# The reciprocal of attention's row sums by way of DRAM, and the first norm's squares summed on VectorE

## The chip, the cores and the metric

The kernel runs on one NeuronCore of a Trainium2 chip. The metric is the device time of one execution in microseconds (us). A NeuronCore has a matrix engine (TensorE, PE in the rows; its weight loads are listed as PEld), VectorE (DVE), ScalarE (ACT), GpSimd (POOL) and SyncE (SP), which here only issues DMAs. Each engine works through its own instructions in order and waits on semaphores for the others.

## The reference

Two layers of a transformer-like trunk over 512 latent and 256 context tokens of width 1024. What matters here:

- Each layer begins with an RMS norm over the 1024 channels, x / sqrt(mean(x^2) + eps), scaled and shifted per channel by values that a matrix product makes from a conditioning vector (the modulation).
- One projection feeds three mixers: a gated delta rule in chunks (GDN), grouped-query attention with 8 heads of 64 channels and 2 key heads, and a short convolution. Their outputs are joined and projected back.
- Attention is softmax(q k^T / 8) v: the exponentials of a row are divided by their sum.
- Then comes a second norm with a SwiGLU network (layer 0) or experts (layer 1).

## The kernel before, in words

Activations lie with channels on partitions and tokens along the free dimension. Most products are made of three matmuls over a high and a low part of each operand (`parts`, `split`: L207 on ACT, L208 on DVE). A framework writes the order of each engine's instructions when the kernel is built: it walks them by priority, which is the order of the program, with its own estimates of durations, and places an instruction when its inputs and its buffer are free by these. On the chip that order is fixed. A load that is placed on SP ahead of another one is issued ahead of it, and one that waits (for a buffer, or for data) holds everything behind it on SP.

**First stage** (`start`, L444 to L492). SP loads modulation weights (groups 2 and 3), the eight tiles of x (128 channels by 768 tokens each), more modulation weights (groups 0 and 1) and the first projection weights. `stats` (L325) sums the squares of a segment of tokens over channels: even tiles are squared on ACT (L339), odd ones on DVE (L337), each square is summed over its 128 partitions by a matmul with ones into four strips of PSUM (L341), the strips are copied (L344), transposed and added up (L347). `rsq` (L234) makes the reciprocal root in 12 small DVE instructions (L239 to L246), and a diagonal matrix times ones (L352, L357) spreads the result over all partitions. `start` runs this for the 512 latent tokens (L479), scales the first 256 of them (`scaled`, L362 on DVE), runs it for the 256 context tokens (L481), and then for each half of the channels makes the modulation (`mod`: L265 on PE) and shifts (`shifted`: L367 on ACT, L368 on DVE). The rest of the tokens follows, and then the first projection (L221 to L223 on PE).

The kernel has a second way to norm, used further on: `square` (L370) squares on ACT and adds on GpSimd into an accumulator (k = 0 and, with two accumulators, k = 7 are written directly), and `rms` (L380) sums the accumulator with one-column matmuls (L387) into PSUM, from which `rsq` reads.

**Attention** (`Mix.attention`, L1496) runs as a generator beside GDN: both are woven together so that attention's work fills PE. The unit is two heads of one pair of query tiles (2 x 128 queries): 12 units in layer 0, 8 in layer 1. `scores` (L1560) makes for each of the two heads and two tiles the scores S (L1572, L1573), the row minimum of the negated scores on DVE (L1574) and the exponentials with their sums on ACT (L1575); the sums lie in `st[:, 1]`, one number per query on its partition, four columns for two heads and two tiles. One unit later `turn` transposes the exponentials (L231, copies L1531), and `values` multiplies with v (L1546); the result has the channels of two heads on the partitions and the queries along the free dimension. So 1 / sum, which is made per query on partitions, is needed along the free dimension, on all 64 partitions of its head. Before, this went over PE: DVE takes the reciprocal (L1535), GpSimd spreads it on four diagonals (L1536), PE multiplies ones with them (L1549) into the second half of the same PSUM bank, ACT copies this to `a_rs` (L1552), and DVE multiplies (L1553, into `a_y`). After that product the bank is free for the next transposes (there are two banks "t").

What else goes through the queues in these stages: in layer 0 six groups of modulation (4 to 9) are made between the units, each with four loads of 512 KB on SP (L196) through three buffers and with L265 on PE. In layer 1 SP has no loads in the attention stage until the output weights. GpSimd issues the loads of q, k, v and of GDN's right sides (L1878).

Of the kernel before, what the change touches and what calls it, by code (L numbers as in the profile page):

```python
# [8 lines left out]
F32 = mybir.dt.float32  # L9
F32R = mybir.dt.float32r  # L10
I32 = mybir.dt.int32
AF = mybir.ActivationFunctionType
# [5 lines left out]
SEGS = ((0, 512), (512, 256))  # L18
# [118 lines left out]
class K:  # L137
# [75 lines left out]
    def mm3(self, out, wh, wl, xh, xl, start, stop):  # L213
        mm = self.nc.tensor.matmul
        mm(out, wh, xh, start=start, stop=False)  # L215
        mm(out, wh, xl, start=False, stop=False)  # L216
        mm(out, wl, xh, start=False, stop=stop)  # L217

    def mm3x(self, out, xh, xl, wh, wl, start, stop):
        mm = self.nc.tensor.matmul  # L220
        mm(out, xh, wh, start=start, stop=False)  # L221
        mm(out, xl, wh, start=False, stop=False)  # L222
        mm(out, xh, wl, start=False, stop=stop)  # L223
# [143 lines left out]
        self.nc.scalar.activation(a, t, AF.Identity, bias=sh)  # L367
        self.nc.vector.scalar_tensor_tensor(b, t, sh, a.bitcast(F32), op0=OP.add, op1=OP.subtract)  # L368

    def square(self, pool, acc, xs, k):  # L370

        nc = self.nc
        if k == 0 or k == 7 and len(acc) > 1:
            nc.scalar.activation(acc[k // 7], xs, AF.Square)
            return
        sq = pool.tile([128, 512], F32, name="sq")[:, :xs.shape[-1]]
        nc.scalar.activation(sq, xs, AF.Square)
        nc.gpsimd.tensor_add(acc[0], acc[0], sq)

    def rms(self, pool, acc, n, b, dg=None):  # L380

# [50 lines left out]
def pools(k, l):  # L432

    def opener(side):
        return lambda es, n, bufs=1: es.enter_context(k.tc.tile_pool(name=n, bufs=bufs, side=side, reuse_waits="tile"))
    r = [opener("left"), opener("right")]
    return r if l == 0 else r[::-1]


def htiles(pool):  # L440
    return [[pool.tile([128, T], F32R, name=f"h{x}{i}") for i in range(8)] for x in "hl"]


def start(k):  # L444
    nc = k.nc
    pa, pb = pools(k, 0)
    eh = ExitStack()
    hh, hl = htiles(pa(eh, "hp"))
    with ExitStack() as es:
        np_ = pb(es, "np", 2)  # L450
        k.weights(es, 0, pb, 12)
        k.banks(es, pn=4, ps=2, pt=2)
        k.mod_begin(0, "pt")
        for g in (2, 3):
            k.mod(0, g, "ps", "pt")
        gain = k.gains(0, 0)
        x = []
        for i in range(8):
            t = np_.tile([128, T], F32, name=f"x{i}", bufs=1)
            nc.sync.dma_start(t, k.xsrc[0][:, i])  # L460
            x.append(t)
        sh = [np_.tile([128, 2, 4], F32, name=f"sh{g}", bufs=1) for g in range(2)]
        rs = {}

        def scaled(s, c, n):
            o = SEGS[s][0]
            for i in range(8):
                k.scaled(x[i][:, o + c:o + c + n], x, s, o + c, n, gain, rs[s][:, c:c + n], i)

        def shifted(s, c, n, ks=range(8)):  # L470
            o = SEGS[s][0] + c
            for i in ks:
                k.shifted(x[i][:, o:o + n], hh, hl, s, o, n, sh[i // 4], -4 * (i // 4), i)

        def mod(g):
            k.mod(0, g, "ps", "pt")
            nc.vector.tensor_copy(sh[g], k.modc[0][:, :, 4 * g:4 * g + 4])

        rs[0], = k.stats(np_, x, SEGS[:1])  # L479
        scaled(0, 0, 256)  # L480
        rs[1], = k.stats(np_, x, SEGS[1:])  # L481
        for g in range(2):
            mod(g)
            shifted(0, 0, 256, range(4 * g, 4 * g + 4))
        ep = ExitStack()
        k.weights(ep, 5, pa, 2)
        w0 = group_weights(k, 0, 1)
        scaled(0, 256, 256)
        shifted(0, 256, 256)
        scaled(1, 0, CTX)  # L490
        shifted(1, 0, CTX)
    return hh, hl, eh, ep, w0  # L492
# [47 lines left out]
def group_weights(k, l, i):  # L540
    n = 2 * WGN[i]
    return [k.weight(k.A[f"wg{i}"][l, q].rearrange("p k n -> p (k n)"), n) for q in range(4)]
# [794 lines left out]
class Mix:  # L1337
# [158 lines left out]
    def attention(self, sp, cat, groups):  # L1496

        k, nc = self.k, self.k.nc
        w, late, n = self.w, None, 0
        for g in range(2):  # L1500
            kh, v = self.first if g == 0 else self.keys(g)
            for h in (4 * g, 4 * g + 2):
                q = self.queries(h) if h else self.q0
                yb = sp.tile([128, w], F32, name="a_y", bufs=1)
                for pair in range(2 if self.last else 3):
                    kts = list(range(NT)) if pair < 2 else [4, 5]
                    st = sp.tile([128, 3, 4], F32, name="a_st", bufs=3)
                    P, pt = [], []
                    for i in range(2):
                        P.append(self.scores(sp, q[i], kh, pair, kts, st, 2 * i))  # L1510
                        if late:
                            self.turn(sp, i, *late)
                        if late and i:
                            self.values(sp, cat, *late)
                        yield
                        n += 1
                        if groups and n % 3 == 0:
                            k.mod(0, groups.pop(0), "t", "t")
                    late = h, pair, kts, P, v, yb, st, pt
        for i in range(2):  # L1520
            self.turn(sp, i, *late)
        self.values(sp, cat, *late)

    def turn(self, sp, j, h, pair, kts, P, v, yb, st, pt):

        k, nc = self.k, self.k.nc
        pt.append(sp.tile([128, NT, 256], F32, name="a_pt"))
        for a in range(0, len(kts), 2):
            tp = k.transposes([P[j][i][:, b * 128:b * 128 + 128] for b in (a, a + 1) for i in range(2)], b="t")
            tp = tp.rearrange("p (t q) -> p t q", t=2)  # L1530
            (nc.vector.tensor_copy if DVE_COPY[self.l] and a == 2 else nc.scalar.copy)(pt[j][:, kts[a]:kts[a] + 2], tp)  # L1531
        if j:

            dg = sp.tile([128, 4, 128], F32, name="a_dg", bufs=1)
            nc.vector.reciprocal(st[:, 2], st[:, 1])  # L1535
            nc.gpsimd.tensor_mul(dg, k.C("ident").unsqueeze(1).to_broadcast([128, 4, 128]),  # L1536
                                 st[:, 2].unsqueeze(2).to_broadcast([128, 4, 128]))
            pt.append(dg)

    def values(self, sp, cat, h, pair, kts, P, v, yb, st, pt):  # L1540

        k, nc, w = self.k, self.k.nc, self.w
        op = k.psum("t")
        for a, t in enumerate(kts):
            for j in range(2):
                nc.tensor.matmul(op[64 * j:64 * j + 64, :256], v[:, t], pt[j][:, t], start=a == 0, stop=a == len(kts) - 1,  # L1546
                                 tile_position=(0, 64 * j))
        for j in range(2):
            nc.tensor.matmul(op[64 * j:64 * j + 64, 256:], k.C("ones")[:, :64],  # L1549
                             pt[2][:, 2 * j:2 * j + 2].rearrange("p i q -> p (i q)"), start=True, stop=True, tile_position=(0, 64 * j))  # L1550
        rs = sp.tile([128, 256], F32, name="a_rs", bufs=1)
        nc.scalar.activation(rs, op[:, 256:], AF.Copy)  # L1552
        nc.vector.tensor_mul(yb[:, pair * 256:pair * 256 + 256], op[:, :256], rs)  # L1553
        if pair == (1 if self.last else 2):
            if 2 + h // 2 in cat:
                k.parts(yb[:, :w], *cat[2 + h // 2])
            else:
                nc.gpsimd.dma_start(self.cat[2 + h // 2, :, :w], yb[:, :w])
# [21 lines left out]
class Gdn:  # L1580
# [64 lines left out]
    def norm(self):  # L1645

        k, nc, ss = self.k, self.k.nc, self.ss
        k.rsq(self.p0, ss, [128, 2, NT, 4], 1.0, EPS, ss, "g")
        nc.vector.tensor_scalar(ss[:, 1], ss[:, 1], 0.125, None, op0=OP.mult)
        for w in range(2):  # L1650
            tok = self.tk[w]
            nc.vector.tensor_mul(tok, tok, ss[:, w].unsqueeze(3).to_broadcast([128, NT, 4, 64]))
            nc.gpsimd.dma_start(self.tok[1 - w], tok)
# [326 lines left out]
```

## Time and profile before

| | us |
|---|---|
| runs, median of 3 | 2132.27 (2132.15, 2132.27, 2135.34) |
| profiled execution | 2134.24 |
| its span in the profile | 2132.5 |
| PE busy | 2011.8 (94%) |
| DVE busy | 1398.4 (66%) |
| ACT busy | 996.0 (47%) |
| POOL busy | 229.5 (11%) |

How to read the rows further down. A row of the timeline gives start and length in us from the span's start, the engine, the line, the operation, what it writes and reads, how many instructions were merged, and in brackets how long the engine had been idle and what ended that. A row of a table of stretches gives the stretch, its length, then the busy time (and the number of instructions) of PE, PEld, DVE, ACT and POOL, the granted clock of PE as a share of 2.4 GHz, the busy share of the DMA engines and GB/s. A row of waits gives who waited for whom, us in total, times, and the longest. A row of one line gives the count, the shortest, median and longest ns, and the first and last start. A row of groups gives count, busy us, mean ns, and the idle time before. SPq is SP's queue. A matmul in full precision is shown as two instructions.

### The profile page before, as it was taken

Reading aid. Unit: us, or ns where it says so; the run is one execution under the profiler, and the core shown is the slowest. Engines: PE = TensorE matmul, PEld = TensorE weight load, DVE = VectorE, ACT = ScalarE, POOL = GpSimd, SP = SyncE. Lnnn points to the kernel's source line nnn. Section 1 sums busy time; section 2 is a strip of 40 time slices with the busy share of each in tenths; the row PEclk is TensorE's granted clock in tenths of the full one; section 3 lists DMA queues with packets and bytes.
Section 4 is the critical chain, followed back from the end, with each engine's and each line's share of the span. In section 5 each row is a group of like instructions: output and inputs, shape, how many; then the busy total and the mean of one; then the engine's idle time right before and its main releaser. Section 6 shows DMA issues by size and latency. Waiting matters only on the chain. (4 is left out here: it accounts for less than half of the span.)

```text
span 2132.5 us, 33501 instructions
## 1 busy us (share of the span) xinstructions
PE 2011.8 (94%) x12422; PEld 1647.2 (77%) x12422; DVE 1398.4 (66%) x2501; ACT 996.0 (47%) x1748; POOL 229.5 (11%) x276
## 2 busy tenths in 40 slices
PE   6999899989999999999989998999789999999996
PEld 2998766768788888888879886778567777777774
DVE  3858855765896734242367598677576788666777
ACT  3665375543322222222246556654365576645555
POOL 0000222214000000000040004210110000000011
PEclk9999999999999999999999999999899999999998
DMA  6342543152564715131233333034597799667674
GB/s 260 93 134 70 166 163 115 33 172 93 197 207 129 246 42 206 33 102 50 69 123 108 102 102 117 22 117 146 168 327 255 257 353 332 214 222 240 241 277 157
DMA packets 123489, 344.56 MB, mean 162 GB/s; under 512 B 13280, under 2 KB 36816, under 8 KB 123312
## 3 DMA queue, kind: packets, MB, share of 16 engines
q1 hardware_dynamic: 81216, 273.85, 38.3%
q0 software_dynamic: 14608, 47.87, 6.7%
q10 hardware_dynamic: 27488, 20.52, 3.1%
q8 instruction: 106, 1.74, 0.3%
q14 instruction: 71, 0.58, 0.1%
HBM read 306.00 MB, written 36.19 MB: 160 GB/s over the span
## 5 line engine op out<-in xcount | busy, mean ns | idle before, releaser
L207 ACT ACTIVATE hi<-raw 128x1024 fp32r<-128x1024 f32 (+3 forms) x444 | 426.2, 987 | 302.2 <-PE ps L216 230.7
L208 DVE TENSOR_TENSOR lo<-raw,hi 128x1024 fp32r<-128x1024 f32 (+2 forms) x432 | 482.7, 1138 | 85.5 <-ACT hi L207 69.5
L215 PE MATMUL ps<-hh,hi 128*128 128x512 f32 (+1 forms) x1040 | 355.8, 342 | 0.8 <-ACT hi L207 0.8
L217 PE MATMUL ps<-hh,lo 128*128 128x512 f32 (+1 forms) x1040 | 353.9, 340 | 1.7 <-DVE lo L208 1.7
L216 PE MATMUL ps<-hl,hi 128*128 128x512 f32 (+1 forms) x1040 | 354.6, 341 | 0.0
L215 PEld LDWEIGHTS ps<-hh,hi 128*128 128x128 f32 x1040 | 198.2, 191 | 26.7 <-ACT hi L207 3.4
L217 PEld LDWEIGHTS ps<-hh,lo 128*128 128x128 f32 x1040 | 198.1, 190 | 24.2 <-DVE lo L208 2.5
L216 PEld LDWEIGHTS ps<-hl,hi 128*128 128x128 f32 x1040 | 198.3, 191 | 21.2
L223 PE MATMUL ps<-lo,xh 128*128 128x512 f32 (+1 forms) x384 | 150.6, 393 | 10.7 <-DVE lo L208 5.1
L221 PE MATMUL ps<-hi,xh 128*128 128x512 f32 (+1 forms) x384 | 145.9, 380 | 2.0 <-ACT hi L207 1.9
L222 PE MATMUL ps<-hi,xl 128*128 128x512 f32 (+1 forms) x384 | 144.7, 377 | 0.0
L1332 DVE TENSOR_TENSOR sg<-sg,ps 128x512 f32<-128x512 f32 (+1 forms) x44 | 24.4, 554 | 150.7 <-PE ps L217 150.7
L217 PE MATMUL ps<-gh,lo 128*128 128x256 f32 (+1 forms) x352 | 119.2, 338 | 2.8 <-DVE lo L208 2.8
L216 PE MATMUL ps<-gl,hi 128*128 128x256 f32 (+1 forms) x352 | 120.2, 342 | 0.0
L215 PE MATMUL ps<-gh,hi 128*128 128x256 f32 (+1 forms) x352 | 119.2, 339 | 0.0
L223 PEld LDWEIGHTS ps<-lo,xh 128*128 128x128 f32 x384 | 72.4, 189 | 38.7 <-DVE lo L208 16.5
L296 DVE SCALAR_TENSOR_TENSOR macc<-mraw,sT,macc 128x512 f32<-128x512 f32 x126 | 89.4, 749 | 13.7 <-DMA mraw<-wmod 12.8
L221 PE MATMUL ps<-hi,hh 128*128 128x400 f32 (+2 forms) x272 | 91.7, 338 | 1.3 <-ACT hi L207 1.1
L223 PE MATMUL ps<-lo,hh 128*128 128x400 f32 (+2 forms) x272 | 89.3, 330 | 0.6 <-DVE lo L208 0.6
L222 PE MATMUL ps<-hi,hl 128*128 128x400 f32 (+2 forms) x272 | 88.4, 326 | 0.0
L1574 DVE TENSOR_REDUCE a_st<-S 128x1 f32<-128x768 f32 (+1 forms) x80 | 66.2, 844 | 31.2 <-PE S L1573 30.8
L1575 ACT ACTIVATE a_p<-S,a_st 128x768 f32<-128x768 f32 (+1 forms) x80 | 65.1, 816 | 43.3 <-DVE a_st L1574 38.9
(594 smaller groups left out, 4140.4 us busy)
## 6 DMA issues: line engine op xcount, KB each, us to landing
raw<-wmg SPq DMA_DIRECT2D x176, 512.0 KB
raw<-wmd SPq DMA_DIRECT2D x80, 512.0 KB
raw<-wmod SPq DMA_DIRECT2D x48, 512.0 KB
mraw<-wmod SPq DMA_DIRECT2D x48, 512.0 KB
raw<-wgu SPq DMA_DIRECT2D x44, 512.0 KB
raw<-wout SPq DMA_DIRECT2D x32, 512.0 KB
raw<-wt SPq DMA_DIRECT2D x24, 512.0 KB
raw<-wd SPq DMA_DIRECT2D x32, 256.0 KB
```

The source lines that it names most:

```text
L207: self.nc.scalar.activation(hi, src, AF.Copy)
L208: (eng or self.nc.vector).tensor_sub(lo, src, hi.bitcast(F32))
L215: mm(out, wh, xh, start=start, stop=False)
L216: mm(out, wh, xl, start=False, stop=False)
L217: mm(out, wl, xh, start=False, stop=stop)
L221: mm(out, xh, wh, start=start, stop=False)
L222: mm(out, xl, wh, start=False, stop=False)
L223: mm(out, xh, wl, start=False, stop=stop)
L296: nc.vector.scalar_tensor_tensor(a, w, c, a, op0=OP.mult, op1=OP.add)
L1332: nc.vector.tensor_mul(s, s, pu)
L1574: nc.vector.tensor_reduce(st[:, 0, c + i:c + i + 1], s[:, :n], axis=AX.X, op=OP.min)
L1575: nc.scalar.activation(P[:, :n], s[:, :n], AF.Exp, bias=st[:, 0, c + i:c + i + 1], scale=-1.0, accum_out=st[:, 1, c + i:c + i + 1])
```

## The change

In attention the reciprocals of a unit are taken as soon as its scores are done, written to a row in DRAM (two heads of 256 queries) and read back twice, each head's row to the 64 partitions of that head. All three DMAs are issued by SP. The diagonal, its matmuls and the copy fall away. In `start` the latent and the context norm are made by `square` and `rms`, with the additions on VectorE in place of GpSimd, and the context's norm stands behind the first shifts.

```diff
-    def square(self, pool, acc, xs, k):
+    def square(self, pool, acc, xs, k, eng=None):
...
-        nc.gpsimd.tensor_add(acc[0], acc[0], sq)
+        (eng or nc.gpsimd).tensor_add(acc[0], acc[0], sq)
...
-        rs[0], = k.stats(np_, x, SEGS[:1])
+        def norm(s):
+            o, n = SEGS[s]
+            acc = [np_.tile([128, 512], F32, name=f"nac{i}")[:, :n] for i in range(2)]
+            for i in range(8):
+                k.square(np_, acc, x[i][:, o:o + n], i, nc.vector)
+            rs[s] = k.rms(np_, acc, n, "pn")
+
+        norm(0)
         scaled(0, 0, 256)
-        rs[1], = k.stats(np_, x, SEGS[1:])
         for g in range(2):
             mod(g)
             shifted(0, 0, 256, range(4 * g, 4 * g + 4))
+        norm(1)
...
-                    late = h, pair, kts, P, v, yb, st, pt
+                    late = h, pair, kts, P, v, yb, self.sums(sp, st, h, pair), pt
...
+    def sums(self, sp, st, h, pair):
+
+        k, nc = self.k, self.k.nc
+        nc.vector.reciprocal(st[:, 2], st[:, 1])
+        row = k.dram.tile([2, 256], F32, name=f"rs{self.l}_{h}_{pair}")
+        nc.sync.dma_start(row.rearrange("j (i p) -> p (j i)", p=128), st[:, 2])
+        rs = sp.tile([128, 256], F32, name="a_rs", bufs=3)
+        for j in range(2):
+            nc.sync.dma_start(rs[64 * j:64 * j + 64], row[j].partition_broadcast(64))
+        return rs
+
-    def turn(self, sp, j, h, pair, kts, P, v, yb, st, pt):
+    def turn(self, sp, j, h, pair, kts, P, v, yb, rs, pt):
...
-        if j:
-
-            dg = sp.tile([128, 4, 128], F32, name="a_dg", bufs=1)
-            nc.vector.reciprocal(st[:, 2], st[:, 1])
-            nc.gpsimd.tensor_mul(dg, k.C("ident").unsqueeze(1).to_broadcast([128, 4, 128]),
-                                 st[:, 2].unsqueeze(2).to_broadcast([128, 4, 128]))
-            pt.append(dg)
-
-    def values(self, sp, cat, h, pair, kts, P, v, yb, st, pt):
+
+    def values(self, sp, cat, h, pair, kts, P, v, yb, rs, pt):
...
-        for j in range(2):
-            nc.tensor.matmul(op[64 * j:64 * j + 64, 256:], k.C("ones")[:, :64],
-                             pt[2][:, 2 * j:2 * j + 2].rearrange("p i q -> p (i q)"), start=True, stop=True, tile_position=(0, 64 * j))
-        rs = sp.tile([128, 256], F32, name="a_rs", bufs=1)
-        nc.scalar.activation(rs, op[:, 256:], AF.Copy)
         nc.vector.tensor_mul(yb[:, pair * 256:pair * 256 + 256], op[:, :256], rs)
```

## Rows read from the trace of the kernel before

**Rows 1.** The page's head and busy time of each engine over the span.

```profile
span 2132.5 us, 33501 instructions
...
PE 2011.8 (94%) x12422; PEld 1647.2 (77%) x12422; DVE 1398.4 (66%) x2501; ACT 996.0 (47%) x1748; POOL 229.5 (11%) x276
```

**Rows 2.** Table of stretches: attention in layer 0 and in layer 1.

```profile
255.00:440.00 185.00, 174.06 (x1634) 126.03 (x1634) 111.67 (x235) 107.88 (x256) 44.61 (x59) 0.99 0.32 109
1298.00:1444.00 146.00, 136.59 (x1425) 108.60 (x1426) 109.39 (x229) 94.72 (x204) 34.79 (x49) 0.98 0.22 69
```

**Rows 3.** Waits of PE in 255 to 440 us, then in 1298 to 1444 us.

```profile
PE S L1572 <- ACT a_p L1575: 6.5, 4, 4.3
...
PE t L231 <- DVE a_y L1553: 0.5, 1, 0.5
```

**Rows 4.** Table of stretches: two of the first stage.

```profile
39.00:52.30 13.30, 10.86 (x74) 5.81 (x74) 12.96 (x47) 9.49 (x22) 0.12 (x1) 1.00 0.15 41
...
55.00:58.40 3.40, 3.40 (x16) 3.22 (x15) 3.40 (x9) 1.17 (x3) 0.10 (x1) 0.51 0.64 218
```

**Rows 5.** Single lines over the whole span: ones times diagonal, the copy, the diagonal.

```profile
L1549 PE MATMUL t<-a_dg,cst x80: 379/379/430, 278.5 to 1440.9; 128*64 128x256 f32 x80
...
L1552 ACT ACTIVATE a_rs<-t x20: 383/384/385, 279.6 to 1441.4; 128x256 f32<-128x256 f32 x20
...
L1536 POOL TENSOR_TENSOR a_dg<-cst,a_st x20: 1033/1040/1124, 263.9 to 1422.3; 128x512 f32<-128x512 f32 x20
```

**Rows 6.** Timeline of one unit's values on PE, layer 0.

```profile
326.72 2.81 PE L1546 MATMUL t<-a_pt,a_v 128*64 128x256 f32 x24
...
329.14 0.36 PEld L1549 LDWEIGHTS t<-a_dg,cst 128*64 128x64 f32 x4
...
329.89 0.16 PEld L265 LDWEIGHTS t<-raw,sT 128*32 128x32 f32 x8 [0.38 <-issue]
```

**Rows 7.** DMA issues: count, KB each, median us from issue to landing.

```profile
r<-tok POOLq DMA_DIRECT2D x24, 128.0 KB, 2.7
...
ids<-tid,slots POOLq DMA_INDIRECT x8, 12.4
```

**Rows 8.** Timeline of DVE: reciprocal and product of one unit, layer 0, layer 1.

```profile
275.10 0.17 DVE L1535 RECIPROCAL a_st<-a_st 128x4 f32<-128x4 f32 x1
...
288.54 0.42 DVE L1553 TENSOR_TENSOR a_y<-t,a_rs 128x256 f32<-128x256 f32 x1 [3.16 <-ACT a_rs L1552]
...
1299.95 0.17 DVE L1535 RECIPROCAL a_st<-a_st 128x4 f32<-128x4 f32 x1
...
1309.08 0.41 DVE L1553 TENSOR_TENSOR a_y<-t,a_rs 128x256 f32<-128x256 f32 x1
```

**Rows 9.** SP's waits (255 to 440 us) and timeline, with PE's wait for its load.

```profile
SPq L196 <- PE t L265: 99.8, 11, 22.4
...
330.98 5.30 SPq L196 DMA_DIRECT2D raw<-wmod  x4
...
334.86 0.14 PEld L265 LDWEIGHTS t<-raw,sT 128*32 128x32 f32 x4 [0.56 <-DMA raw<-wmod]
...
374.89 0.33 SPq L196 DMA_DIRECT2D raw<-wmod  x1
...
1421.30 46.88 SPq L196 DMA_DIRECT2D raw<-wout  x13
```

**Rows 10.** First norm's timeline, a later norm's column matmuls, DVE's context squares (groups).

```profile
24.41 0.62 ACT L339 ACTIVATE sq<-x 128x512 f32<-128x512 f32 x1
...
25.86 0.68 DVE L337 TENSOR_TENSOR sq<-x 128x512 f32<-128x512 f32 x1
...
34.72 0.17 DVE L239 TENSOR_SCALAR rqxs<-ss 128x4 f32<-128x4 f32 x1
...
507.60 1.64 PEld L387 LDWEIGHTS pn<-cst,nac 128*128 128x128 f32 x14
...
L337 DVE TENSOR_TENSOR sq<-x 128x256 f32<-128x256 f32 x4 | 1.7, 423 | 1.4 <-PE pn L341 1.4
```

## The prediction

> **What bounds the kernel now.** The page comes first: TensorE is busy 94% of the span, VectorE 66%, ScalarE 47%, GpSimd 11%, and the profiled execution took 2134.24 us of which 2132.5 are span [rows 1]. A change must therefore take time from PE's queue or from a stretch in which PE stands. The table of stretches comes next, for the two stages that the change touches. In attention (255 to 440 us for layer 0, 1298 to 1444 us for layer 1) PE is busy 174.06 of 185 and 136.59 of 146 us, while DVE and ACT are busy 58 to 75%: PE sets the pace, and only 10.9 + 9.4 us of these 331 are gaps [rows 2]. The list of PE's waits says what fills the gaps: in layer 0 mostly the exp of the next scores (6.5 us), while the chain that the change rewrites (sums, copy, product) costs PE 0.5 us of waiting in layer 1 and less in layer 0 [rows 3]. In the first 60 us it is the other way round. PE has little work there, and between 39.0 and 52.3 us DVE is busy 12.96 of 13.3 us: DVE scales and shifts the normalised x and PE waits for it; from 55.0 to 58.4 us the granted clock is 0.51, the lower level of 1.2 GHz, after the stretch in which PE had waited [rows 4].
>
> **The change, part by part.**
>
> *Attention, removed from PE.* Each of 20 units (12 in layer 0, 8 in layer 1) loses the product of ones with the spread diagonal, four matmul instructions, 80 in all [rows 5]. Their mean of 0.38 us is a pipelined latency, not a price: pairs overlap. The price is the spacing: 24 instructions of the same shape take 2.81 us from first start to last end, so (2.81 - 0.38) / 23 = 0.106 us each, and the four of a unit 0.42 us [rows 6]. 80 x 0.106 = 8.5 us, all on the engine that sets the pace. Lower end: 0, if the sequence of scans and exps sets the end. Upper end: from the first weight load of the four at 329.14 to the next work's at 329.89 is 0.75 us [rows 6], 20 x 0.75 = 15.0 with the gap behind them. I take 8.5, because PE is busy 94% of both windows.
>
> *Attention, removed elsewhere.* ACT loses 20 copies of 0.38 us and POOL 20 products of 1.04 us [rows 5]. Neither sets the pace, so both count nothing. The copy's end now falls out between the last value matmul and the release of the PSUM bank, which is worth at most those 0.5 us of PE's waits for a_y and their like in layer 0 [rows 3]; I leave it out.
>
> *Attention, added.* The reciprocal stays, one DVE instruction of 0.17 us, and only moves ahead. Three DMAs per unit are new, all on SP: 128 x 4 numbers to a row in DRAM, then two reads spread over 64 partitions each, which wait on SP for the row to land. Nothing of just this shape is in the trace. The nearest DMA of a few KB to 128 KB, r from tok, lands 2.7 us after issue; the farthest one, ids, which also puts single 4-byte numbers into DRAM but with indices and from POOL, needs 12.4 us [rows 7]. I take 2.7 for either hop, since the row has no indices; with three issues of some 0.33 us [rows 9] that is 2.7 + 2.7 + 1.0 = 6.4 us from reciprocal to 1 / sum in place. What covers it is the distance from a unit's reciprocal to its product: 13.4 us at the shortest in layer 0 (275.10 to 288.54) and 9.1 us in layer 1 (1299.95 to 1309.08) [rows 8]. Covered, so nothing. If the write took the 12.4 us of ids, the chain would be 16.1 us, and those two units would come 2.7 and 7.0 us late.
>
> On this the Trainium skill speaks against the change: "DMA: Bandwidth & Descriptors", in its rules for kernel authors, says that a last dimension that isn't contiguous becomes one descriptor per element and should be rearranged. The row's write is of that kind, 512 pieces of 4 bytes, and no run shows this shape yet. By that rule the sum would hold the late units of the sentence before; by the row of r it holds none. What it would do to the time is the second rival.
>
> *SP's queue.* While a unit's reads wait for the row, SP can issue nothing else: 2.7 us and the issues, about 3.4 us a unit. In layer 1 SP's weight loads begin only at 1421.30, so nobody waits before. In layer 0 it loads the modulation's weights, six groups of four loads through three buffers, so that a group's last load goes out late: issued from 330.98, PE stands for it at 334.86, after 0.56 us of waiting [rows 9]. Twelve holds of 3.4 us are 41 of 185 us, so one or two of the six groups meet one, seldom a whole one: between 0 and 6 x 3.4 = 20 us, of which I take 1.0, less than one full hold. The row can be held as well, by loads that wait on SP for a free buffer: that is a rival.
>
> *First norm.* For the 512 latent columns ACT and DVE made four squares each, and eight pairs of matmuls summed them, then a copy and four transposes: first square at 24.41, reciprocal root from 34.72 us [rows 10]. Now ACT makes all eight squares, DVE adds six at 0.69 us. DVE is free for them at 25.86, where its first square stood, so 25.86 + 6 x 0.69 = 30.0. Then 16 column matmuls follow; 14 of them take 1.64 us in layer 0's later norm, so 16 take 1.9 [rows 10]. The root starts at about 32.2 instead of 34.72: 2.5 us earlier, and with it the scaling behind it. The context's norm moves behind the first shifts: on DVE four squares of 0.42 us leave the full stretch and six adds of 0.42 us come [rows 10], which can fall into the gaps ahead of 39 us, where DVE now has them. At worst they stay in the full stretch: 2 x 0.42 = 0.84 us lost. At best squares and nine or more root steps leave it, about 3.5 us more. A second stretch at 1.2 GHz like that of [rows 4] would cost half of 3.4 = 1.7 us, and without the present one 1.7 come back. So the ends are -2.5 - 3.5 - 1.7 = -7.7 and -2.5 + 0.84 + 1.7 = 0.0. I take -2.5: DVE bounds this stretch before and after, and its total hardly falls.
>
> *Sum.* -8.5 + 1.0 - 2.5 = -10.0 us against the profiled execution's 2134.24, so 2124.2. The median of the runs, 2132.27, lies 1.97 us lower; in its terms **2122.3**, rounded to 2122. Ends of the terms: -15.0 - 7.7 = -22.7 (2110) and 0 + 20 + 0 (2152).
>
> **The rivals.**
>
> *The time goes into waits* (0.13). PE's order is fixed, and behind the removed matmuls stands work that waits for ACT's exp, already 6.5 us in layer 0 [rows 3]. If half of the 8.5 us turns into such waits and the first norm gains nothing, the change is -4.2 + 1.0 = -3.2: 2129, no change. For it: DVE's full stretch in the first stage; against it: the gaps of PE are only 6%.
>
> *The row's write is slow* (0.06). Its 512 pieces land after the 12.4 us of ids, and the products of the two units with the shortest cover come 2.7 + 7.0 = 9.7 us late, with DVE and then PE behind them: 2122.3 + 9.7 = 2132, no change. For it: pieces of the same 4 bytes. Against it: ids goes by indices, r without. This is what the rule of the Trainium skill on a last dimension that isn't contiguous, cited above, would mean here.
>
> *1 / sum stands on SP, and the kernel is slower* (0.13). The row is queued behind a load that waits for PE to free its buffer. In layer 0 SP waited 99.8 us in 11 such waits, the longest 22.4 us [rows 9]. A row behind that one is in place 22.4 + 6.4 us after its reciprocal, 28.8 - 13.4 = 15.4 us late where the cover is shortest; DVE stands at the product in order, the score maxima behind it, then exp and PE. One such unit gives 2122.3 + 15.4 = 2137.7, and that is where it begins to decide; each more adds up to as much. For it: one queue for loads and rows. Against it: those waits end with matmuls that PE passes in the same order as the scores, so that a row mostly finds its place between the groups of loads.
>
> *The change does what it says, and gains* (0.68), the forecast.
>
> **How the numbers follow.** A measurement of this kernel can tell about 0.2%, 4.3 us, from no change: faster is below 2128, slower above 2136.5. Faster has 0.68, same 0.19, slower 0.13. Same is the first two rivals, slower the third. The range goes from 2113, nine below the forecast: the best ends of both parts together are unlikely, either alone (-6.5 and -5.2 against what I take) is inside. It ends at 2134, which takes in the first two rivals and leaves out the third.
>
> **What would show it.** Right: no matmul on the ones, PE busy in the attention stages about 8 us less with their length falling alike; the product on DVE without a wait for a_rs; the reciprocal root's first step at about 32 us and the scaling at about 36.5. Wrong: a wait of DVE's product for a DMA of several us, PE waiting longer for the modulation's weights, attention stages as long as before with more idle PE, or matmuls of the first projection that start no earlier than 47 to 52 us.

## The result, and the profile after

The changed kernel is **slower**: 2187.37 us (median of 4 runs, 2185.1 to 2188.76) against 2132.21 of the kernel before on the same chip, ratio 1.0258, 95% interval 1.024 to 1.0277. The forecast was 2122. The lines below answer to the groups ahead of the prediction; lines moved a little, so that L1559 is now DVE's product with 1 / sum, L1578/L1579 are the scores, L1581 the exp, L1536 the row's write and L1539 its two reads (in e5 below, L1539 and L1541).

First the page's head [rows 1], then the table of stretches for the two attention stages [rows 2]:

```profile
span 2185.9 us, 33350 instructions
...
PE 2015.5 (92%) x12328; PEld 1651.7 (76%) x12328; DVE 1395.8 (64%) x2503; ACT 993.0 (45%) x1734; POOL 208.2 (10%) x256
```

```profile
255.00:440.00 185.00, 140.83 (x1109) 94.62 (x1109) 75.31 (x151) 78.69 (x177) 19.92 (x32) 0.82 0.49 96
1298.00:1444.00 146.00, 126.96 (x1058) 100.50 (x1056) 108.40 (x199) 82.50 (x163) 28.64 (x39) 0.94 0.39 84
```

PE has fewer instructions and yet as much busy time. In layer 0 it now stands for 44 of 185 us (11 before), and its granted clock falls from 0.99 to 0.82. The DMA engines are busier (0.49 against 0.32) and move less (96 against 109 GB/s). That last pair is the one to stop at: more DMA time for fewer bytes.

In fixed points of the program: from the first scores of layer 0 to its first residual addition (DVE's `xr`, L737, after the joined projection), 219.5 us became 267.8 (246.8 to 514.6). From there to the last such addition of layer 1 it is 1039.8 us (to 1554.4), where it was 1029.0, about 11 more. So the loss is in layer 0's attention stage first of all. What PE waited for there, in 255 to 440 us, and then in layer 1 (1298 to 1480 us) [rows 3]:

```profile
PE t L265 <- DMA raw<-wmod: 34.8, 5, 9.3
PE S L1578 <- ACT a_p L1581: 4.4, 1, 4.4
```

```profile
PE t L231 <- DVE a_y L1559: 6.6, 1, 6.6
```

Five of the six groups of modulation weights came late, 7 us each on average; before it was one, by 0.56 us [rows 9]. SP's waits in 255 to 440 us, and a piece of SP's timeline, show the first suspect [rows 9]:

```profile
SPq L1539 <- DMA rs<-a_st: 78.7, 9, 10.0
...
SPq L196 <- PE t L265: 14.7, 6, 4.3
```

```profile
380.62 1.09 SPq L1539 DMA_DIRECT2D a_rs<-rs  x2
381.82 6.32 SPq L196 DMA_DIRECT2D raw<-wmod  x4
391.41 0.38 SPq L1536 DMA_DIRECT2D rs<-a_st  x1
399.44 1.09 SPq L1539 DMA_DIRECT2D a_rs<-rs  x2
```

Between the row's write at 391.41 and the reads at 399.44 SP does nothing but wait for 2 KB to land: 8.7 us a time (78.7 / 9), where I had taken 2.7. DVE's product then waits for 1 / sum in two units of this window and in one of layer 1 (1285 to 1500 us) [rows 8]:

```profile
DVE a_y L1559 <- DMA a_rs<-rs: 13.4, 2, 9.2
```

```profile
DVE a_y L1559 <- DMA a_rs<-rs: 8.3, 1, 8.3
```

But the time from issue to landing has also grown where SP has no part, in GpSimd's own loads (250 to 480 us; `r` was 2.7 [rows 7], `a_q` 3.4):

```profile
r<-tok POOLq DMA_DIRECT2D x12, 128.0 KB, 5.0
...
a_q<-qs POOLq DMA_DIRECT2D x4, 384.0 KB, 12.0
```

### The profile page after: what moved, and what is told of

Same layout as the page of the kernel before. It is cut to its first block, busy times and chain, and to the rows that moved or that the text cites. A ratio compares the mean times of both kernels' runs of the same rounds, so it can differ in the third digit from the quotient of the medians.

```text
span 2185.9 us, 33350 instructions
## 1 busy us (share of the span) xinstructions
PE 2015.5 (92%) x12328; PEld 1651.7 (76%) x12328; DVE 1395.8 (64%) x2503; ACT 993.0 (45%) x1734; POOL 208.2 (10%) x256
## 5 line engine op out<-in xcount | busy, mean ns | idle before, releaser
L217 PEld LDWEIGHTS ps<-hh,lo 128*128 128x128 f32 x1040 | 197.6, 190 | 23.2 <-DVE lo L208 1.7
L296 DVE SCALAR_TENSOR_TENSOR macc<-mraw,sT,macc 128x512 f32<-128x512 f32 x126 | 89.0, 745 | 14.7 <-DMA mraw<-wmod 14.2
L1581 ACT ACTIVATE a_p<-S,a_st 128x768 f32<-128x768 f32 (+1 forms) x80 | 65.1, 815 | 51.9 <-DVE a_st L1580 49.3
```

What stands on the lines that cost most here:

```text
L296: nc.vector.scalar_tensor_tensor(a, w, c, a, op0=OP.mult, op1=OP.add)
L1581: nc.scalar.activation(P[:, :n], s[:, :n], AF.Exp, bias=st[:, 0, c + i:c + i + 1], scale=-1.0, accum_out=st[:, 1, c + i:c + i + 1])
```

## The experiments

The first theory was SP's queue: the write lands late, SP stands for it, and the loads behind it are late. Its rival: the write itself holds up all other transfers, whoever waits for it. A third question was what each half of the change is worth.

**Halves of the change.** e1_norm_only is the kernel before with the new first norm, e2_att_only the kernel before with attention's part.

> The kernel before with the new first norm alone; attention as before. If the whole loss lies in attention (either theory below), this gains what the traces show between the first stage and the first scores of layer 0: 251.5 to 246.8 us, so about 2132.2 - 4.7 = 2127.5 us. If the loss came from a woven order that the first norm's new place upsets everywhere, it would be slower than 2132 us.

> The kernel before with attention's change alone; the first norm as before. The first norm alone gave 0.9999, so if the parts add up this is as slow as the whole change, ratio 1.024 to 1.028. Its first stage is that of before, so its first scores of layer 0 tell where that stage ends in another execution: at about 251.5 us if the first norm really gains the 4 to 5 us that the traces of the new norm show, at 247 us if the one trace of before was a late one.

Measured: the norm alone 2131.23 us, ratio 0.9999 (0.9986 to 1.0011); attention alone 2184.58, 1.0237 (1.02 to 1.0274). No gain of the norm is seen (its interval allows 3.0 us of gain to 2.3 of loss), and the loss is attention's. Why the norm gives so little is seen in the changed kernel. Stretch 24 to 39 us, the kernel before and then after, then PE's and DVE's timeline after [rows 4, 10]:

```profile
24.00:39.00 15.00, 10.23 (x40) 2.71 (x44) 6.54 (x23) 3.94 (x7) 0.98 (x2) 1.00 0.85 335
```

```profile
24.00:39.00 15.00, 8.13 (x32) 4.75 (x32) 9.29 (x29) 7.49 (x17) 1.04 (x3) 0.66 0.82 322
```

```profile
30.10 3.57 PE L387 MATMUL pn<-cst,nac 128*128 128x1 f32 x16 [5.39 <-DVE nac L378]
```

```profile
33.71 0.16 DVE L239 TENSOR_SCALAR rqxn<-pn 128x4 f32<-128x4 f32 x1 [3.33 <-PE pn L387]
33.79 0.43 DVE L378 TENSOR_TENSOR nac<-nac,sq 128x256 f32<-128x256 f32 x1
...
39.53 1.66 DVE L362 SCALAR_TENSOR_TENSOR x<-x,gain,pn 128x256 f32<-128x256 f32 x4 [1.22 <-PE pn L392]
```

PE, which had summed the squares, now stands 5.39 us for DVE's additions; the granted clock of the stretch is 0.66 instead of 1.00, that is partly at 1.2 GHz (0.50 from 30.10 to 33.67 us); and the 16 column matmuls, which fall into just that part, take 3.57 us, not 1.9. The context's additions (33.79 and five like it) stand between the steps of the root. Counted from the first square, the root begins after 9.8 us (10.3 before) and the scaling after 15.6 (14.7 before): half a microsecond won, one lost. The first projection's first matmul comes 22.8 us after the first square (46.73 - 23.90), before 23.2 (47.58 - 24.41): 0.3 us is left. The first scores of layer 0 stand 4.7 us earlier in this trace than in that of the kernel before, but that is mostly not the norm's: with the old norm they come 227.2 us after the first square in the trace of the kernel before and 223.6 in e2's (248.40 us), with the new one 223.0.

**Longer pieces, same queue and waits.** e3_pieces16 writes the row as 128 pieces of 16 bytes (each partition's four numbers side by side); the reads are as in the change, so that the numbers which divide belong to other queries. e5_pe_row turns the four columns on PE and writes four pieces of 512 bytes.

```diff
-        nc.sync.dma_start(row.rearrange("j (i p) -> p (j i)", p=128), st[:, 2])
+        nc.sync.dma_start(row.rearrange("j (p c) -> (j p) c", c=4), st[:, 2])      # e3
...
+        tp = k.transposes([st[:, 2]], w=4, b="t")                                   # e5
+        nc.scalar.copy(rs[:4, :128], tp[:4, :128])
+        nc.sync.dma_start(row.rearrange("j (i p) -> (j i) p", p=128), rs[:4, :128])
```

> The changed kernel with the row written as 128 pieces of 16 bytes in place of 512 of 4 bytes; the reciprocals then lie in the row in another order, so each query is divided by another query's sum. Queue theory (SP stands behind the row's landing and the modulation loads come late): if the landing goes with the number of pieces, it falls from 9 us to about 4, SP's wait per unit alike, PE's wait for raw from 35 us to under 10, and 30 to 45 of the 55 us come back: 2142 to 2157 us. If the landing is a fixed time of a write to DRAM, it stays at 9 us and the time at 2187. Late-product theory (DVE stands at the product for a_rs): only its 22 us of waits come back, 2165 us.

> The changed kernel with the unit's 4 x 128 reciprocals turned by one transpose on PE and copied by ACT, so that the row is written as 4 pieces of 512 bytes; the result is the same. Queue theory with the landing set by the number of pieces: landing about 2 to 3 us, PE's wait for raw near that of before, layer 0's stage about as short as before, 2125 to 2135 us in all. With a fixed landing time: about 2187 us. Late-product theory: no wait for a_rs, 22 us back, 2165 us.

Measured: e3 2120.33 us, ratio 0.9945 (0.9932 to 0.9957); e5 **2114.57**, 0.9924 (0.9907 to 0.9942), faster than both kernels. SP's waits in 255 to 440 us, e3 and then e5:

```profile
SPq L1539 <- DMA rs<-a_st: 21.6, 11, 3.2
```

```profile
SPq L1541 <- DMA rs<-a_rs: 13.5, 12, 2.3
```

SP waits 2.0 and 1.1 us a time instead of 8.7. PE's wait for the modulation's loads is 4.2 us in e3, 2.9 in e5. The route over DRAM is sound; the 4-byte pieces are not.

**Is it SP's wait?** e6_const_row keeps the write but lets the reads take a row of ones that was stored beforehand, so that nobody waits for the landing; the division is left out. e7_write_only is the kernel before, with the old diagonal, and a write of 512 x 4 bytes that nobody reads; in e8_write_only_act ACT issues it. e9_sums_pool is the changed kernel with write and reads on GpSimd.

```diff
+            row = k.dram.tile([2, 256], F32, name=f"rs{self.l}_{len(self.rows)}")
...
+            nc.sync.dma_start(row.rearrange("j (i p) -> p (j i)", p=128), st[:, 2])   # e7; e8: nc.scalar
```

> The changed kernel, with the row still written as 512 pieces of 4 bytes, but the two reads of a unit take a row of ones that was written once ahead, so that SP doesn't wait for the landing; the division by the sums is left out. Queue theory: SP's wait is the cause, not the write itself: PE's wait for raw falls to a few us and the time to 2120 to 2135 us, with the removed matmuls' 8.5 us and the first norm's 4.7 us visible. If the writes themselves disturb (16 DMA engines busy with small pieces), the loads stay slow and the time stays over 2160 us.

> The kernel before, its 1 / sum by way of PE, with the row's write added on SP in 512 pieces of 4 bytes; nobody reads the row. Theory that SP's wait for the landing is the harm: SP waits only for the reciprocal, so 2131 to 2137 us. Theory that the pieces themselves hold up the loads that are issued behind them on the same queue: PE waits for raw 15 us or more in layer 0 and the time is 2145 to 2165 us. Late-product theory: no change at all.

> The same useless write, issued by ACT instead of SP. If the pieces hold up only what is behind them on their own queue: PE's wait for raw as in the kernel before (under 2 us), 2131 to 2140 us, the rest being ACT's own stops for the reciprocal. If they hold up the 16 DMA engines for everyone: as slow as the write on SP, 2145 us or more.

> The changed kernel with the row's write and its two reads issued by GpSimd. SP then has loads alone: if the loss is that of SP's queue, whichever part of it, PE's wait for raw falls to 2 us or less and the layer 0 stage comes back to 185 us, unless GpSimd's own waits make GDN's right sides late: 2118 to 2140 us. If 1 / sum is late (the landing from GpSimd as slow as that of ids, 12.4 us), DVE's product waits for a_rs some 20 us in all and the time is 2135 to 2155 us.

Measured: e6 2165.74 us, ratio 1.0149 (1.0124 to 1.0174); e7 2191.51, 1.0279 (1.0252 to 1.0305); e8 2191.37, 1.0269 (1.0237 to 1.0301); e9 2178.34, 1.0222 (1.0196 to 1.0248). A write without any reader, beside the complete old kernel, costs as much as the whole change, and as much from ACT as from SP. The first theory, SP's wait, falls as the main cause. The Trainium skill ("DMA: Bandwidth & Descriptors", Issuing engines are not separate DMA queues) says that transfers of all issuers end on the same 16 DMA engines and interleave; the runs agree: from SP and ACT the same write cost the same (2191.51 and 2191.37 us), and with write and reads on GpSimd most of the loss stayed (2178.34).

The table of DMA queues shows it: packets, MB, and their time as a share of 16 engines' span. In 250 to 480 us, q0 is GpSimd's queue, q10 ACT's, q1 SP's. The kernel before, then e8, then PE's waits of e8 in the same window:

```profile
q1 hardware_dynamic: 4428, 16.17, 20.5%
q0 software_dynamic: 2736, 9.83, 13.6%
```

```profile
q0 software_dynamic: 2320, 8.00, 24.4%
q1 hardware_dynamic: 3136, 11.40, 15.1%
q10 hardware_dynamic: 6336, 0.03, 1.4%
```

```profile
PE t L265 <- DMA raw<-wmod: 23.4, 5, 7.5
```

The 4-byte pieces on q10 (12 writes of 512, and semaphores) take 1.4% themselves. But GpSimd's loads took 13.6% for 9.83 MB before, 1.38% a MB, and take 24.4 / 8.00 = 3.05% a MB now: packets on *another* queue last 2.2 times as long. SP's packets hardly lengthen in e8 (20.5 / 16.17 = 1.27% a MB before, 15.1 / 11.40 = 1.32%), but SP's loads land late: the first load of each of five groups of modulation weights, issued 2 to 4.4 us behind a write, has its last packet done 7.4 to 9.3 us after its issue, where before it was 2.8 to 3.1. The records of single packets say how GpSimd's loads are slowed. In e8 the 512 pieces of a write begin within about 0.4 us (median of 20 writes) and are booked with 9 ns each; what grows is the tail of ordinary packets behind them. All 109 packets of more than 2 us counted for e8 below begin within 8.3 us behind the start of a write:

```
GpSimd's queue, packets of 3 KB and more, 250 to 480 us (ns, rounded down)
                        count  median  99th pct  longest  over 2 us
before                   2176     234       760     2075          1
e8   512 x 4 bytes       1856     211      4870     7573        109
e12  512 x 16 bytes      2176     232       644      955          0
e13  128 x 4 bytes       2112     234      3432     6284         81
e14  4 bytes, 1 KB off   2176     221       612     2928          1
e18  4 bytes, 8 off      2176     232       724     2218          5
e19  2 bytes, 4 off      2112     234      3363     5980         87
```

**What makes such a piece dear: number, size, neighbours?** Nine more kernels are e7 with another useless write in its place; eight of them here, and e19 writes 2 bytes of each number, 4 bytes apart:

```diff
+  row.rearrange("j (p c) -> (j p) c", c=4), st[:, 2]                               # e11: 128 x 16 bytes
+  row.rearrange("i p c -> p i c"), st[:, 2].unsqueeze(1).to_broadcast([128, 4, 4]) # e12: 512 x 16
+  row[0, :128].rearrange("(p c) -> p c", c=1), st[:, 2, :1]                        # e13: 128 x 4
+  row[:, :1], st[:, 2, :1]                         # e14: 128 x 4, row [128, 256], so 1 KB apart
+  row[0].rearrange("(p c) -> p c", c=2), st[:, 2, :2]                              # e15: 128 x 8
+  row[:, :, 0], st[:, 2]                           # e16: 512 x 4, row is an SBUF tile [128, 4, 2]
+  row[0, 8:264].rearrange("(p c) -> p c", c=2), st[:, 2, :2]                       # e17: 128 x 8, shifted
+  row[0].rearrange("(p c) -> p c", c=2)[:, :1], st[:, 2, :1]                       # e18: 128 x 4, 8 apart
```

> The kernel before, with a row that nobody reads, written by SP as 128 pieces of 16 bytes (2 KB, as many bytes as in the run with 512 pieces of 4, at the same places of SP's queue). If each piece costs by its count (about 59 us / 10,240 pieces), a quarter of the pieces costs 15 us: 2147. If pieces of 4 bytes are what costs, nothing: 2132, and PE's wait for the modulation's loads (20 to 35 us with 512 x 4) is under 4 us. If any extra DMA at these places costs, by its issue or by its wait on SP for the reciprocal, 2187 to 2191 again.

> The kernel before, with a row of four times the bytes that nobody reads, written by SP as 512 pieces of 16 bytes. By the count of pieces: as much as 512 x 4, 2187 to 2191, with a landing of some 8 us behind which raw<-wmod comes late. By the size of a piece (4 bytes alone cost): 2132. Between the two if both count.

> The kernel before, with 128 numbers that nobody reads, written by SP as 128 pieces of 4 bytes. By the count of pieces: 2147, like 128 x 16. By the size of a piece: a quarter of the 59 us as well, 2147, where 128 x 16 gives 2132. If only a long write blocks the others (each write lands before the next load is due), under 2136.

> The kernel before, with 128 numbers that nobody reads, written by SP as 128 pieces of 4 bytes that lie 1 KB apart in DRAM. If a piece of 4 bytes costs by itself: as the 128 neighbouring ones, 2150 to 2160, PE waiting some 11 us for raw. If what costs is that neighbouring pieces, moved by different DMA engines, write into one short stretch of DRAM: 2132, like 16-byte pieces.

> The kernel before, with 256 numbers that nobody reads, written by SP as 128 pieces of 8 bytes. If only 4-byte pieces are special: 2132. If the cost falls with the size of a piece: between 2135 and 2156. If every piece under 16 bytes costs the same: 2156, as 128 x 4.

> The kernel before, with the 512 reciprocals moved by SP as 512 pieces of 4 bytes to another tile in SBUF that nobody reads, in place of DRAM. If the cost lies in writing 4 bytes to DRAM: 2132. If it lies in moving 4-byte pieces anywhere: 2187 to 2191, with GpSimd's queue at over 20% again.

> The kernel before, with 128 pieces of 8 bytes as in the run before, but beginning 32 bytes into the row. If pieces cost where two DMA engines write into one and the same short block of DRAM (with pieces of 8 bytes from the row's start each engine would have blocks of its own, shifted by 32 bytes it would share them): 2145 to 2160. If 8 bytes are free wherever they lie: 2130 to 2132.

> The kernel before, with 128 pieces of 4 bytes, 8 bytes apart, so that they lie over the same 1 KB as the 128 pieces of 8 bytes that cost nothing. If what costs is the number of pieces in one short block of DRAM or the sharing of a block by two engines: 2130 to 2132. If a piece of 4 bytes near others costs by its size: 2150 to 2160.

> The kernel before, with 128 pieces of 2 bytes, 4 bytes apart, over the same 512 bytes as the 128 pieces of 4 bytes that cost 24 us. If what costs is how many pieces fall into one short stretch of DRAM (as many here as there, twice as many as with the pieces 8 bytes apart): 2150 to 2160. If it needs pieces of 4 bytes that touch each other: 2130 to 2132.

| run | pieces | bytes from start to start | us | ratio (95%) |
|---|---|---|---|---|
| e7 | 512 x 4 | 4 | 2191.51 | 1.0279 (1.0252 to 1.0305) |
| e13 | 128 x 4 | 4 | 2155.87 | 1.0112 (1.0089 to 1.0134) |
| e19 | 128 x 2 | 4 | 2157.66 | 1.0127 (1.0099 to 1.0155) |
| e18 | 128 x 4 | 8 | 2129.78 | 0.9997 (0.9985 to 1.0009) |
| e15 | 128 x 8 | 8 | 2130.16 | 0.9993 (0.9983 to 1.0004) |
| e17 | 128 x 8, shifted 32 bytes | 8 | 2130.70 | 1.0004 (0.9991 to 1.0017) |
| e11 | 128 x 16 | 16 | 2131.62 | 1.0003 (0.9992 to 1.0014) |
| e12 | 512 x 16 | 16 | 2132.85 | 1.0007 (0.9994 to 1.0019) |
| e14 | 128 x 4 | 1024 | 2128.80 | 0.9987 (0.9973 to 1.0001) |
| e16 | 512 x 4, to SBUF | 8 | 2132.09 | 0.9999 (0.9985 to 1.0014) |

The number of pieces falls (e12), and so does their size alone (e14, e18). What the dear ones have in common is that they begin 4 bytes apart in DRAM: e19, with the same density and pieces that do not touch, costs as much as e13. Queue times and landings (250 to 480 us) go with it, and in e13 SP's packets lengthen as well (26.6 / 14.55 = 1.83% a MB); e13's queues, then e14's, then the landing in e15 and in e19:

```profile
q1 hardware_dynamic: 5727, 14.55, 26.6%
q0 software_dynamic: 2656, 9.44, 20.5%
```

```profile
q1 hardware_dynamic: 6157, 16.11, 20.5%
q0 software_dynamic: 2736, 9.83, 13.1%
```

```profile
rs<-a_st SPq DMA_DIRECT2D x12, 1.0 KB, 2.8
```

```profile
rs<-a_st SPq DMA_DIRECT2D x12, 0.2 KB, 8.5
```

256 bytes in 128 pieces land after 8.5 us, 1 KB in as many pieces after 2.8. The sharing of a short block by two engines, which e17 was made for, found no support. e16 tells less than it was meant to: its pieces lie 8 bytes apart, which is free in DRAM too, so SBUF as a target of pieces 4 bytes apart stays untried. What happens in the memory at that density is open as well; nothing between 4 and 8 bytes was tried, and no reads in such pieces.

**The best version with the old norm.** e10_pe_row_old_norm is e5 without the change of the first norm.

> The version whose row is turned by one PE transpose and written as 4 pieces of 512 bytes (2114.6 with the new first norm), here with the first norm of before. If the first norm is worth nothing: 2114 to 2116. If the new first norm still saves its 2.5 us behind a row that costs nothing: 2117.

Measured: 2116.75 us, ratio 0.9941 (0.9925 to 0.9957); the interval overlaps with e5's. The gain is attention's, and which norm stands in front cannot be told at this size. The page's head of e5, against [rows 1]:

```profile
span 2113.0 us, 33432 instructions
...
PE 1995.0 (94%) x12348; PEld 1639.6 (78%) x12348; DVE 1393.9 (66%) x2503; ACT 997.2 (47%) x1754; POOL 208.8 (10%) x256
```

## Why the prediction was wrong, step by step

*What bounds the kernel.* Right: PE sets the pace, and once the write is harmless the removed matmuls show as time (e5: PE busy 2011.8 to 1995.0, span 2132.5 to 2113.0).

*Attention, removed from PE.* Mechanism right, size too small. The forecast took 8.5 us by the spacing of the matmuls and gave 15.0 as the upper end, with the gap behind them. The ratios of e10 and e5 give 0.59% and 0.76% of 2132, 13 and 16 us, even after e5 and e10 put one transpose and one copy a unit back. The whole stretch from the first of these matmuls to the next work, 0.75 us a unit [rows 6], fits that better than the spacing; no run takes these matmuls out by themselves.

*Attention, added.* **This is the step that failed**: "I take 2.7 for either hop, since the row has no indices ... Covered, so nothing." The hop took 8.7 us, and the worse error was to price it only as a delay of its own readers. The delay itself was of the kind that the rival of the slow write worked out, at about twice its size: three products late by 21.7 us together (13.4 + 8.3), against 9.7 in two. But the same pieces lengthen GpSimd's packets and make SP's loads land late, which no step and no rival had, and which costs more. With nobody waiting for the landing (e6) the kernel is still 1.49% = 32 us slower; as matmuls worth 13 to 16 us or more are gone there too, the writes alone are worth some 45 to 48 us. The wait for the landing would be the rest of the change's 2.58% = 55 us: 55 - 32 = 23 us. By e7, where the writes beside the old kernel cost 59 us, it would be only 55 - 59 + 13 to 16 = 9 to 12. These are differences of runs, not single waits, and the parts do not simply add up; that the writes are the larger part holds by both. The rule of the Trainium skill that stood beside this step ("DMA: Bandwidth & Descriptors", Rules for kernel authors: one descriptor per element) named the right place, and the forecast gave it 0.06. As a measure of harm the rule is too wide: e14 and e18 too move each number as a piece of its own, 1 KB or 8 bytes apart, and cost nothing. So is that page's Specifications row, by which transfers under 512 bytes are read, modified and written back: pieces of 8 and 16 bytes showed no cost here.

*SP's queue.* "Twelve holds of 3.4 us ... one or two of the six groups meet one", 1.0 us, at most 20. The holds were 8.7 us and more, the loads behind them were themselves slowed, and five of six groups came late, 34.8 us of PE's waiting. In e8, where SP does not hold at all, it is still 23.4.

*The clock in the attention stage.* Left out altogether in this part of the prediction. The stretch of layer 0's attention, from the first scores to the first residual addition, in the kernel before, after, and in e7:

```profile
251.50:471.00 219.50, 202.00 (x1814) 147.91 (x1813) 136.80 (x297) 122.36 (x283) 51.15 (x66) 0.98 0.38 124
```

```profile
246.80:514.60 267.80, 213.94 (x1765) 153.16 (x1764) 135.55 (x296) 118.56 (x271) 38.06 (x54) 0.87 0.50 108
```

```profile
248.20:517.40 269.20, 224.46 (x1812) 164.31 (x1811) 137.29 (x296) 122.79 (x283) 51.12 (x66) 0.88 0.45 101
```

PE's standing grew from 219.5 - 202.0 = 17.5 to 267.8 - 213.9 = 53.9 us, 36.4 of the 48.3 lost; the other 11.9 are busy time, and that with fewer matmuls, at a granted clock of 0.87 instead of 0.98. In e7, with the very matmuls of before, the split is 27 of standing and 22.5 of slower work; by estimate the clock alone would make 202.00 x 0.98 / 0.88 = 225 us of the busy time of before, and 224.46 is what e7 shows. Whoever prices PE's waits must price the work behind them too.

*First norm.* Taken at -2.5; by the trace 0.3 us is left of it at the first projection, and e1's time shows no gain, though its interval does not exclude 2.5. "16 take 1.9" was read from a stretch in which PE was busy, at a granted clock of 1.00; here it had stood, the clock was 0.50, and they took 3.57. The steps of the root, 2.3 us before, took 3.9 with the context's additions between them. The term's upper end, 0, was about right, and one reason given for it (a second stretch at 1.2 GHz) is what the row shows.

*The third rival* (1 / sum behind a load on SP) had the sign but not the mechanism: SP's waits for a free buffer fell from 99.8 us to 14.7, and the row was late by itself: 18 of the 20 writes were issued within 0.4 us of their reciprocal. Of the marks named for a wrong forecast, three appeared: DVE's product waiting for a DMA of several us, PE waiting for the modulation's weights, and more idle PE in the attention stages, which even grew longer.

## What to carry to other kernels

A transfer of few bytes is not cheap because it is small or because its reader has time: ask how its pieces lie in DRAM, and who else is moving data. One number per partition, written side by side to DRAM, should first be turned on chip or stored with gaps; here one PE transpose of four columns turned a loss of 55 us into a gain of 13 to 16. When DMA's busy share rises while GB/s falls, compare the time per MB of queues that have nothing to do with the edit: that view found the culprit where the chain of waits named its victims.

## What the runs showed that had not been expected

128 writes of 4 bytes, beginning 4 bytes apart in DRAM, cost a kernel with 20 such DMAs 24 us (1.0112); the same pieces 8 bytes apart cost nothing (0.9997). Their own records last 9 ns; it is ordinary packets behind them, GpSimd's above all, that last up to 6.3 us (7.6 with the 512 pieces of e8). And the cost is less than proportional: four times as many pieces (e7) cost 59 us, not 96.
